# Attention blocks gathered into one stream with one PSUM bank per head, and the first two w_out_2 tiles begun together

## The chip, the cores and the metric

The kernel runs on one core of one Trainium2 chip. The metric is the device time of one execution in microseconds (us); three runs of the kernel before are shown, and one execution of it was profiled.

## What is computed

A decoder of 512 tokens and width 1024. Two layers of a first block (a feed-forward, a mixer, a feed-forward), then one layer of a second block (a mixer, a feed-forward) and a norm. The first block's mixer has, beside a pooling branch, two causal attentions of six heads each: MLA, and FoX, whose scores get a bias from a forget gate. The second block's mixer has a dilated window attention of six heads in three groups, an RWKV7 and a state space branch; their outputs are gated, summed and multiplied by `w_out_2`. Cut to what the change touches:

```python
def causal_block_attention(q, k, v, scale, log_decay_cum=None):
    def one_block(args):                     # blocks of 128 queries
        i, q_blk = args[0], args[1]
        sc = jnp.einsum('bhqd,bhkd->bhqk', q_blk, k) * scale
        if log_decay_cum is not None:
            sc = sc + c_blk[..., :, None] - log_decay_cum[..., None, :]
        sc = jnp.where(kpos[None, :] <= qpos[:, None], sc, -jnp.inf)
        p = jax.nn.softmax(sc, axis=-1)
        return jnp.einsum('bhqk,bhkd->bhqd', p, v)
def dilated_window_attention(q, k, v, window, dilation):
    scores = jnp.where(mask, jnp.einsum('bnqrhe,bnkrhe->bnrhqk', qb, kb) * (e ** -0.5), -jnp.inf)
    mx = jnp.max(scores, axis=-1, keepdims=True)
    p = jnp.exp(scores - mx)
    den = jnp.sum(p, axis=-1, keepdims=True)
    out = jnp.einsum('bnrhqk,bnkrhe->bnqrhe', p / den, vb)
    lse = mx + jnp.log(den)
merged = gates[0] * y_attn + gates[1] * y_rwkv + gates[2] * y_ssm
h = h + merged @ w_out
```

## The kernel before

Activations lie feature by feature: tiles of 128 features by 512 tokens. A weight matrix product is done for 128 output features at a time over eight k tiles of 128. Each float32 operand is split in a high and a low fp32r part, and `mm3` (lines 201 to 203) issues three matmuls for each k tile: high by high, high by low, low by high. These are the "main" matmuls, 128x512 with 128 rows. `load_w` (L394) brings a weight tile by DMA on SyncE's queue, casts its high part on ScalarE (L404) and takes the low part as a difference on VectorE (L406). There are two slots for split weights. `gemm_stream` (L410) does the output tiles one after the other; its argument `ahead=(i0, n)` lets the tiles i0 and i0+1 each do their first n k tiles before either goes on. The mixers of the first block use it; the last mixer doesn't.

The order of instructions is set when the program is built. `Sched` (L55) is a planner: every piece of work is a stream that yields an engine ("P" TensorE, "V" VectorE, "A" ScalarE, "G" GpSimd) and a cost, takes and returns slots (`acq`, `rel`: A and B are PSUM banks, s and sT the tiles for scores and turned scores) and waits for events. The piece that can start first, or of those within a short time the one with the lowest priority number, goes next. The weight product stream has priority 50 and fills what attention leaves free. Each engine then runs its instructions in that order and waits by semaphores.

First block: `attn_pair_s` (L569) takes two heads and spawns four streams `attn_block` (L522), one for each block i of 128 queries with kw = 128(i+1) keys. A stream takes two B banks for the scores of its two heads (`scores2`, L519), does `softmax_s` (the causal mask is added on VectorE, L501; the bias is added and the row maximum taken, L503; times -scale, L506; exponential with its sum on ScalarE, L508), then the reciprocal (L541), the scaling by it (L543), the transposes of its 128x128 pieces on TensorE into one B bank (L549), a copy to SBUF (L467 on ScalarE or L469 on VectorE) and the value products (L565), which add up in the pair's A bank:

```python
for j in range(nb):
    b = slice(j * P, (j + 1) * P)
    for e in range(2):
        nc.tensor.matmul(po[e], vt(e, j), sT[e][:, b], start=j == 0, stop=j == nb - 1)
```

Last mixer: `attn2` has a pair of heads in each of three groups, and in each group four streams `iteration` (L1544) of the same form, 256 keys wide in group 0 (the first block 128), 128 wide in groups 1 and 2; transposes are L1567, value products L1583. There the division comes later, so nothing is scaled ahead of the transposes. Three such streams may hold score tiles at a time.

End of the last mixer: the three branches' outputs are gated on VectorE (L1451), summed in two additions on GpSimd (L1462) and split in mgh (L476, ScalarE) and mgl (L478, VectorE), one tile of 128 features for each of eight. The `w_out_2` products take these eight as their k tiles; each output tile is added to the residual x on VectorE (L1047).

Of the kernel before, what the change touches and what calls it, by code (L numbers as in the profile page):

```python
# [9 lines left out]
F32 = mybir.dt.float32  # L10
F32R = mybir.dt.float32r
AF = mybir.ActivationFunctionType
# [141 lines left out]
class Kern:  # L154
# [341 lines left out]
    def softmax_s(self, ps, kw, s, st, bias, scale, diag, ev):  # L496

        nc = self.nc
        if diag is not None:
            yield V2  # L500
            nc.vector.tensor_add(ps[:, kw - P :], ps[:, kw - P :], diag)  # L501
        yield ("V", 0.08 + kw * 0.00104)
        nc.vector.tensor_tensor_reduce(s, ps, bias, 1.0, -3.0e38, ALU.add, ALU.max, st[0])  # L503
        yield ("rel", "B")
        yield V1
        nc.vector.tensor_scalar(st[1], st[0], -scale, None, ALU.mult)  # L506
        yield ("A", 0.28 + kw * 0.00083, 0, self.EXP)
        nc.scalar.activation(s, s, AF.Exp, bias=st[1], scale=scale, accum_out=st[2])  # L508
        yield ("sig", ev)

    def scores2(self, pair, kw, half):

        out = []
        for _ in pair:
            yield ("acq", "B")
            out.append(self.psB()[:, :kw])
        yield ("P", kw * 0.00168 * (1 if half else 2) + (0.2 if half else 0.0))
        for ps, (q, k) in zip(out, pair):
            self.nc.tensor.matmul(ps, q, k, start=True, stop=True)  # L519
        return out  # L520

    def attn_block(self, mp, pair, kw, biases, scale, diags, vt, po, done, prio, own):  # L522

        nc = self.nc
        nb = kw // P
        cs, ct = ("s", "sT") if own else ("sx", "sTx")
        ring = lambda: self.t(self.xp, "xin", (P, T), F32, 16)[:, :kw]
        yield ("acq", cs)
        ss = [self.t(mp, "s", (P, self.w_s), bufs=self.n_s)[:, :kw] if own else ring() for _ in range(2)]
        sts = [self.t(mp, "st", (P, 4), bufs=12) for _ in range(2)]  # L530
        half = pair[0][0].shape[0] == 64
        pss = yield from self.scores2(pair, kw, half)
        soft = Ev(2)

        def head(e):
            st, s = sts[e], ss[e]
            sl = [st[:, n : n + 1] for n in range(4)]
            ev = Ev()
            yield from self.softmax_s(pss[e], kw, s, sl, biases[e], scale, diags[e], ev)
            yield V1  # L540
            nc.vector.reciprocal(sl[3], sl[2])  # L541
            yield ("V", 0.135 + kw * 0.0005)
            nc.vector.tensor_scalar(s, s, sl[3], None, ALU.mult)  # L543
            yield ("acq", "B")
            pt = self.psB()[:, :kw]
            yield ("P", 0.11 * nb)
            for j in range(nb):
                b = slice(j * P, (j + 1) * P)
                nc.tensor.transpose(pt[:, b], s[:, b], self.ident)  # L549
            sT[e] = self.t(mp, "sT", (P, self.w_s), bufs=self.n_sT)[:, :kw] if own else ring()  # L550
            yield from self.copy(sT[e], pt, kw)
            yield ("rel", "B")
            yield ("sig", soft)

        sT = [None] * 2
# [5 lines left out]
        yield ("P", 0.2 + 0.115 * nb * 2)  # L561
        for j in range(nb):
            b = slice(j * P, (j + 1) * P)
            for e in range(2):
                nc.tensor.matmul(po[e], vt(e, j), sT[e][:, b], start=j == 0, stop=j == nb - 1)  # L565
# [3 lines left out]
    def attn_pair_s(self, mp, heads, vt, scale, prio, y, p, ev, own=True):  # L569
# [4 lines left out]
        done = Ev(4)  # L574
        for i in range(4):
            kw = (i + 1) * P
            bs = [bias[:, T - kw :] if diag is None else bias[:, :kw] for _, _, bias, diag in heads]
# [1717 lines left out]
```

## Time and profile before

| | |
|---|---|
| median of 3 runs | 2836.07 us (2832.83 to 2840.84) |
| profiled execution | 2837.68 us, of which the span from the first to the last instruction is 2835.9 us |
| mean granted clock of TensorE | 0.994 |
| TensorE (PE) busy | 2786.9 us, 98% |
| weight loads of TensorE (PEld) | 2220.2 us, 78% |
| VectorE (DVE) busy | 1637.9 us, 58% |
| ScalarE (ACT) busy | 1044.7 us, 37% |
| GpSimd (POOL) busy | 443.4 us, 16% |
| DMA | 277.45 MB, 98 GB/s |

A row of the profile names the engine, the line of the kernel, the operation, and what it writes and reads ("A<-xin,whi": bank tile A from xin and whi). Matmuls run into each other in the array, and the profile shows each with its own length; so two rows overlap, and the distance between two starts tells what one takes from the time. A number in brackets is the idle time ahead of an instruction and what ended it. The attentions of the first block lie at about 398 to 544 us and 1337 to 1487 us, that of the last mixer at 1987 to 2044 us, and its `w_out_2` product begins at 2411.85 us.

### The profile page before, as it was taken

The page shows a single profiled execution, that of the slowest core. Times are in us where ns is not written, and L with a number is a line of the kernel's source. Part 1 is how long each engine was busy: PE and PEld are TensorE (multiplying, and loading weights), DVE is VectorE, ACT ScalarE, POOL GpSimd, SP SyncE. Part 2 cuts the span into 40 slices and gives each one's busy share as a digit, 9 for nine tenths or more (in the row PEclk, how much of TensorE's full clock was granted, in tenths as well). Part 3 has the DMA queues.
Part 4 walks back from the last instruction along what each step waited for, and adds up shares of the span by engine and source line. Part 5 has one row for each costly group of instructions (what it writes and reads, how often), then busy time and mean ns, then how long its engine had stood idle before and what let it go on. Part 6 is the DMA issues. An engine that isn't in the chain of part 4 may idle for free. (4 is left out here: it accounts for less than half of the span.)

```text
span 2835.9 us, 33440 instructions
## 1 busy us (share of the span) xinstructions
PE 2786.9 (98%) x13036; PEld 2220.2 (78%) x13036; DVE 1637.9 (58%) x2557; ACT 1044.7 (37%) x1615; POOL 443.4 (16%) x364
## 2 busy tenths in 40 slices
PE   9999999999999999999999999998999999999998
PEld 7888877788888888887768788885677878788886
DVE  6454566654545554456665745668766756464543
ACT  4222354532223322235464324462325443332223
POOL 1010111010001200012102101124332213210012
PEclk9999999999999999999999999999999999999999
DMA  4223331222232322224123333352231116223222
GB/s 143 97 94 99 106 104 58 79 97 97 96 98 91 103 97 97 97 92 132 55 68 97 104 104 119 110 174 76 86 102 63 46 46 230 89 97 100 94 97 82
DMA packets 91974, 277.45 MB, mean 98 GB/s; under 512 B 11944, under 2 KB 13096, under 8 KB 91816
## 3 DMA queue, kind: packets, MB, share of 16 engines
q1 hardware_dynamic: 91816, 275.32, 29.6%
q8 instruction: 102, 1.67, 0.2%
q14 instruction: 56, 0.46, 0.1%
HBM read 255.87 MB, written 19.40 MB: 97 GB/s over the span
## 5 line engine op out<-in xcount | busy, mean ns | idle before, releaser
L201 PE MATMUL A<-xin,whi 128*128 128x512 f32 x2368 | 941.5, 398 | 5.6 <-ACT whi L151 5.1
L203 PE MATMUL A<-xin,wlo 128*128 128x512 f32 x2368 | 929.0, 392 | 3.6 <-DVE wlo L193 1.9
L202 PE MATMUL A<-xin,whi 128*128 128x512 f32 x2368 | 930.9, 393 | 0.0
L192 ACT CAST whi<-wraw 128x1024 fp32r<-128x1024 f32 (+1 forms) x338 | 347.7, 1029 | 1018.2 <-issue 377.9
L193 DVE TENSOR_TENSOR wlo<-wraw,whi 128x1024 fp32r<-128x1024 f32 (+1 forms) x338 | 498.8, 1476 | 82.4 <-ACT whi L192 60.4
L201 PEld LDWEIGHTS A<-xin,whi 128*128 128x128 f32 x2368 | 446.8, 189 | 118.5 <-issue 23.5
L203 PEld LDWEIGHTS A<-xin,wlo 128*128 128x128 f32 x2368 | 446.7, 189 | 98.1 <-DVE wlo L193 2.7
L202 PEld LDWEIGHTS A<-xin,whi 128*128 128x128 f32 x2368 | 446.8, 189 | 94.0 <-issue 5.3
L343 POOL TENSOR_TENSOR u<-u,g 128x512 f32<-128x512 f32 x110 | 156.4, 1422 | 1431.9 <-DVE u L341 1154.9
L202 PE MATMUL B<-hl,whi 128*128 128x512 f32 x880 | 343.2, 390 | 1.5 <-DVE hl L225 1.3
L203 PE MATMUL B<-hh,wlo 128*128 128x512 f32 x880 | 342.4, 389 | 0.0
L201 PE MATMUL B<-hh,whi 128*128 128x512 f32 x880 | 342.4, 389 | 0.0
L352 DVE SCALAR_TENSOR_TENSOR x<-B,x 128x512 f32<-128x512 f32 x120 | 83.0, 692 | 307.3 <-PE B L203 307.3
L341 DVE TENSOR_TENSOR u<-A,rb 128x512 f32<-128x512 f32 x110 | 76.0, 691 | 255.8 <-PE A L203 255.8
L404 ACT CAST whi<-wraw 128x1024 fp32r<-128x1024 f32 (+2 forms) x117 | 120.0, 1025 | 219.4 <-PE A L202 133.6
L202 PEld LDWEIGHTS B<-hl,whi 128*128 128x128 f32 x880 | 165.2, 188 | 38.2 <-DVE hl L225 4.3
L201 PEld LDWEIGHTS B<-hh,whi 128*128 128x128 f32 x880 | 165.2, 188 | 35.0
L203 PEld LDWEIGHTS B<-hh,wlo 128*128 128x128 f32 x880 | 165.2, 188 | 34.1
L406 DVE TENSOR_TENSOR wlo<-wraw,whi 128x1024 fp32r<-128x1024 f32 (+2 forms) x117 | 155.2, 1327 | 26.6 <-ACT whi L404 26.1
L337 DVE TENSOR_TENSOR g<-A,rb 128x512 f32<-128x512 f32 x110 | 75.9, 690 | 157.4 <-PE A L203 157.3
L274 POOL TENSOR_TENSOR ssum<-ssum,sq 128x512 f32<-128x512 f32 x48 | 79.3, 1653 | 366.2 <-ACT sq L273 359.7
L224 ACT CAST hh<-u 128x512 fp32r<-128x512 f32 x110 | 68.5, 623 | 158.5 <-POOL u L343 158.5
(478 smaller groups left out, 2822.0 us busy)
## 6 DMA issues: line engine op xcount, KB each, us to landing
wraw<-in_f2gu SPq DMA_DIRECT2D x88, 512.0 KB, 3.3
wraw<-in_f1gu SPq DMA_DIRECT2D x86, 512.0 KB, 3.3
wraw<-in_w_in SPq DMA_DIRECT2D x76, 512.0 KB, 3.4
wraw<-in_f3gu SPq DMA_DIRECT2D x44, 512.0 KB, 3.3
wraw<-in_f1db SPq DMA_DIRECT2D x32, 448.0 KB, 3.3
wraw<-in_f2db SPq DMA_DIRECT2D x32, 448.0 KB, 3.3
wraw<-in_w_out SPq DMA_DIRECT2D x24, 512.0 KB, 3.4
wraw<-in_f1da SPq DMA_DIRECT2D x16, 512.0 KB, 3.3
```

The lines of the kernel that those rows point to most:

```text
L192: nc.scalar.copy(hi[:, b], raw[:, b])
L193: nc.vector.tensor_sub(lo[:, b], raw[:, b], hi[:, b])
L201: mm(ps, wh, xh, start=first, stop=False)
L202: mm(ps, wh, xl, start=False, stop=False)
L203: mm(ps, wl, xh, start=False, stop=last)
L274: (nc.vector if k == NK - 1 else nc.gpsimd).tensor_add(self.ssum, self.ssum, sq)
L337: nc.vector.tensor_mul(g, pg, rb)
L341: nc.vector.tensor_mul(u, pu, rb)
L343: nc.gpsimd.tensor_mul(u, u, g)
L352: nc.vector.scalar_tensor_tensor(self.x[o], ps, scale, self.x[o], ALU.mult, ALU.add)
L404: nc.scalar.copy(hi[:, :width], raw[:, :width])
L406: nc.vector.tensor_sub(lo[:, :width], raw[:, :width], hi[:, :width])
```

## The change

First, `attn_block` takes several blocks of queries as one stream. Their scores lie side by side in one bank for each head: blocks 0 and 1 together (128 + 256 columns), block 2 and block 3 alone. Mask, bias and maximum, exponential and scaling remain one instruction for each block; the product with -scale and the reciprocal are done once for the stream; the transposes of all its pieces go into one bank and are copied once (`turned`); the value products of its blocks follow each other. Second, the last mixer's attention does the same: group 0 in two streams of two blocks, groups 1 and 2 in one stream of four blocks each; score tiles become 512 wide, four instead of six, and two streams instead of three may hold them. Third, `gemm_stream` of the last mixer gets `ahead`: the first two w_out_2 tiles do seven k tiles each before either does its eighth. The core of the diff:

```diff
-    def softmax_s(self, ps, kw, s, st, bias, scale, diag, ev):
+    def softmax_s(self, ps, subs, s, sts, scale, diag):
+
 
         nc = self.nc
-        if diag is not None:
-            yield V2
-            nc.vector.tensor_add(ps[:, kw - P :], ps[:, kw - P :], diag)
-        yield ("V", 0.08 + kw * 0.00104)
-        nc.vector.tensor_tensor_reduce(s, ps, bias, 1.0, -3.0e38, ALU.add, ALU.max, st[0])
+        for c, bias, st in subs:
+            kw = c.stop - c.start
+            if diag is not None:
+                yield V2
+                nc.vector.tensor_add(ps[:, c.stop - P : c.stop], ps[:, c.stop - P : c.stop], diag)
+            yield ("V", 0.08 + kw * 0.00104)
+            nc.vector.tensor_tensor_reduce(s[:, c], ps[:, c], bias, 1.0, -3.0e38, ALU.add, ALU.max, st[0])
         yield ("rel", "B")
         yield V1
-        nc.vector.tensor_scalar(st[1], st[0], -scale, None, ALU.mult)
-        yield ("A", 0.28 + kw * 0.00083, 0, self.EXP)
-        nc.scalar.activation(s, s, AF.Exp, bias=st[1], scale=scale, accum_out=st[2])
-        yield ("sig", ev)
-
-    def scores2(self, pair, kw, half):
+        nc.vector.tensor_scalar(sts[1], sts[0], -scale, None, ALU.mult)
+        for c, bias, st in subs:
+            yield ("A", 0.28 + (c.stop - c.start) * 0.00083, 0, self.EXP)
+            nc.scalar.activation(s[:, c], s[:, c], AF.Exp, bias=st[1], scale=scale, accum_out=st[2])
+
+    def scores2(self, pairs, w, half):
...
+        for c, pair in pairs:
+            for ps, (q, k) in zip(out, pair):
+                self.nc.tensor.matmul(ps[:, c], q, k, start=True, stop=True)
...
+    def turned(self, s, w, out):
+
+        yield ("acq", "B")
+        pt = self.psB()[:, :w]
+        yield ("P", 0.11 * w / P)
+        for b in range(0, w, P):
+            self.nc.tensor.transpose(pt[:, b : b + P], s[:, b : b + P], self.ident)
+        t = out()[:, :w]
+        yield from self.copy(t, pt, w)
+        yield ("rel", "B")
+        return t
+
...
+    def attn_block(self, mp, heads, blocks, scale, vt, po, done, prio, own):
...
+        ends = [sum(n + 1 for n in blocks[: x + 1]) * P for x in range(len(blocks))]
+        cols = [slice(e - (n + 1) * P, e) for n, e in zip(blocks, ends)]
+        w = ends[-1]
...
+            n = len(blocks)
+            yield from self.softmax_s(pss[e], subs, s, (st[:, 0, :n], st[:, 1, :n]), scale, diag)
...
+            nc.vector.reciprocal(st[:, 3, :n], st[:, 2, :n])
+            for x, c in enumerate(cols):
+                yield ("V", 0.135 + (c.stop - c.start) * 0.0005)
+                nc.vector.tensor_scalar(s[:, c], s[:, c], st[:, 3, x : x + 1], None, ALU.mult)
...
+            sT[e] = yield from self.turned(s, w, out)
...
+        yield ("P", 0.2 + 0.23 * w / P)
+        for i, c in zip(blocks, cols):
+            for j in range(i + 1):
+                b = slice(c.start + j * P, c.start + j * P + P)
+                for e in range(2):
+                    y = po[e * 64 : e * 64 + 64, i * P : i * P + P]
+                    nc.tensor.matmul(y, vt(e, j), sT[e][:, b], start=j == 0, stop=j == i)
...
-        done = Ev(4)
-        for i in range(4):
+        done = Ev(3)
+        for i, blocks in enumerate(((0, 1), (2,), (3,))):
+            it = self.attn_block(mp, heads, blocks, scale, vt, po, done, prio + 0.02 * i, own)
...
-        self.n_s, self.n_sT, self.w_s, self.p_load = 6, 4, 256, 1.05
+        self.n_s, self.n_sT, self.p_load = 4, 4, 1.05
...
-        sch = self.sch = Sched(self.preload, E2, N2, W2, A=4, B=4, s=3, sT=2, sq=1, zb=4, gt=2, j=2, jx=1, av=2, u=4, q=5, gl=6, B2=2, raw=3, w=2)
+        sch = self.sch = Sched(self.preload, E2, N2, W2, A=4, B=4, s=2, sT=2, sq=1, zb=4, gt=2, j=2, jx=1, av=2, u=4, q=5, gl=6, B2=2, raw=3, w=2)
...
-            sch.add(self.gemm_stream(items), 50, "g")
+            sch.add(self.gemm_stream(items, None if stop else (len(order) + NK, NK - 1)), 50, "g")
...
+            los = [max(0, i - 1) if g == 0 else i for i in blocks]
+            ends = [sum(n - lo + 1 for n, lo in zip(blocks[: x + 1], los)) * P for x in range(len(blocks))]
+            cols = [slice(e - (n - lo + 1) * P, e) for n, lo, e in zip(blocks, los, ends)]
+            w = ends[-1]
...
+                yield from self.softmax_s(pss[s], subs, ts[s], (st[:, s, g, 0, a:b], ng[:, n + a : n + b]), 0.125, None)
+                sT[s] = yield from self.turned(ts[s], w, lambda: self.t(ap, "sT", (P, T), bufs=self.n_sT))
...
+            sets = ((0, 1), (2, 3)) if g == 0 else ((0, 1, 2, 3),)
+            dn = Ev(len(sets))
+            for i, blocks in enumerate(sets):
```

TensorE, first layer, first FoX pair, behind the scores of blocks 0 and 1 (fk, fq: keys and queries; s: scores; sT: turned scores; c_ident: the identity that transposes). Before:

```order
L549 MATMUL B_2890<-c_ident_141,s_2826 128x128 x2
L565 MATMUL A_2819<-sT_2880,vt_2799 64x128
L565 MATMUL A_2819<-sT_2882,vt_2799 64x128
L549 MATMUL B_2895<-c_ident_141,s_2827 128x128 x2
L519 MATMUL B_2905<-fk_2740,fq_2700 128x384
L519 MATMUL B_2906<-fk_2740,fq_2700 128x384
L565 MATMUL A_2819<-sT_2909,vt_2799 64x128
L565 MATMUL A_2819<-sT_2915,vt_2799 64x128
```

Changed:

```order
L533 MATMUL B_2905<-c_ident_141,s_2820 128x128 x3
L533 MATMUL B_2910<-c_ident_141,s_2821 128x128 x3
L533 MATMUL B_2914<-c_ident_141,s_2826 128x128 x3
L533 MATMUL B_2920<-c_ident_141,s_2827 128x128 x3
L201 MATMUL A_2872<-xin_2529,whi_2795 128x512
L202 MATMUL A_2872<-xin_2530,whi_2795 128x512
L203 MATMUL A_2872<-xin_2529,wlo_2796 128x512
L586 MATMUL A_2819<-sT_2918,vt_2799 64x128
L586 MATMUL A_2819<-sT_2924,vt_2799 64x128
```

The four blocks' transposes, value products and scores alternated before; now the transposes of both heads of blocks 0, 1 and 2 stand together, three main matmuls follow, and twelve value products (to A_2819, the first two shown) run without a break up to the scores of block 3. The 384-wide scores of block 2, between the value products before, have moved up behind those of blocks 0 and 1.

TensorE at the first w_out_2 tiles (A_18607 and A_18645 before, A_18319 and A_18351 now; mgh and mgl are the k tiles, mgh_18627 before and mgh_18339 now the eighth). Before:

```order
L201 MATMUL A_18607<-mgh_18586,whi_18563 128x512
L202 MATMUL A_18607<-mgl_18587,whi_18563 128x512
L203 MATMUL A_18607<-mgh_18586,wlo_18564 128x512
L201 MATMUL A_18607<-mgh_18627,whi_18563 128x512
L202 MATMUL A_18607<-mgl_18628,whi_18563 128x512
L203 MATMUL A_18607<-mgh_18627,wlo_18564 128x512
L201 MATMUL A_18645<-mgh_18298,whi_18605 128x512
```

Changed:

```order
L203 MATMUL A_18351<-mgh_18298,wlo_18318 128x512
L201 MATMUL A_18319<-mgh_18339,whi_18275 128x512
L202 MATMUL A_18319<-mgl_18340,whi_18275 128x512
L203 MATMUL A_18319<-mgh_18339,wlo_18276 128x512
L201 MATMUL A_18351<-mgh_18339,whi_18317 128x512
L202 MATMUL A_18351<-mgl_18340,whi_18317 128x512
L203 MATMUL A_18351<-mgh_18339,wlo_18318 128x512
L201 MATMUL A_18401<-mgh_18010,whi_18377 128x512
L202 MATMUL A_18401<-mgl_18011,whi_18377 128x512
L201 MATMUL A_18434<-mgh_18010,whi_18399 128x512
L202 MATMUL A_18434<-mgl_18011,whi_18399 128x512
L203 MATMUL A_18401<-mgh_18010,wlo_18378 128x512
```

Before, the first tile's eighth k tile follows its seventh directly, and the second tile begins behind it. Now the second tile's first seven k tiles stand ahead of the first tile's eighth, and the third and fourth tile (A_18401, A_18434) begin behind the pair.

VectorE, first layer, third FoX pair, blocks 0 and 1 (st: a row's maximum, sum and reciprocal; vm: values in token order). Before:

```order
L541 RECIPROCAL st_3609<-st_3609 128x1
L506 TENSOR_SCALAR st_3616<-st_3616 128x1
L819 TENSOR_TENSOR x_3642<-A_3624,c_rope_2585 128x512
L543 TENSOR_SCALAR s_3607<-s_3607,st_3609 128x128
L469 COPY vm_2604<-B_3649 128x384
L541 RECIPROCAL st_3610<-st_3610 128x1
L541 RECIPROCAL st_3615<-st_3615 128x1
L541 RECIPROCAL st_3616<-st_3616 128x1
L543 TENSOR_SCALAR s_3608<-s_3608,st_3610 128x128
L543 TENSOR_SCALAR s_3613<-s_3613,st_3615 128x256
L543 TENSOR_SCALAR s_3614<-s_3614,st_3616 128x256
```

Changed:

```order
L567 RECIPROCAL st_3577<-st_3577 128x2
L469 COPY vm_2604<-B_3618 128x384
L570 TENSOR_SCALAR s_3575<-s_3575,st_3577 128x128
L570 TENSOR_SCALAR s_3575<-s_3575,st_3577 128x256
L567 RECIPROCAL st_3578<-st_3578 128x2
L469 COPY vm_2604<-B_3632 128x384
L570 TENSOR_SCALAR s_3576<-s_3576,st_3578 128x128
L570 TENSOR_SCALAR s_3576<-s_3576,st_3578 128x256
L506 ISA s_3582,st_3584<-B_3586,cb_3089 128x384
```

The first head's transposes need the scaling of s_3607 before, of both parts of s_3575 now. One copy of vm stood ahead of the second head's first scaling; now there are two, and the second head's scalings (s_3576) follow the first head's second part.

## Rows read from the trace of the kernel before

**Rows 1.** Page, busy time of TensorE: us, share of the span, instructions.

```profile
PE 2786.9 (98%) x13036; PEld 2220.2 (78%) x13036; DVE 1637.9 (58%) x2557; ACT 1044.7 (37%) x1615; POOL 443.4 (16%) x364
```

**Rows 2.** Timeline of TensorE, first w_out_2 tile: start, duration, engine, line, operation.

```profile
2411.85 0.39 PE L201 MATMUL A<-mgh,whi 128*128 128x512 f32 x1
...
2416.38 0.39 PE L203 MATMUL A<-mgh,wlo 128*128 128x512 f32 x1
2419.44 0.50 PE L201 MATMUL A<-mgh,whi 128*128 128x512 f32 x1 [2.67 <-ACT mgh L476]
2420.17 0.49 PE L202 MATMUL A<-mgl,whi 128*128 128x512 f32 x1 [0.23 <-DVE mgl L478]
...
2424.37 0.40 PE L201 MATMUL A<-mgh,whi 128*128 128x512 f32 x1
```

**Rows 3.** Table of waits of TensorE: us in total, times, longest.

```profile
PE B L549 <- DVE s L543: 6.1, 4, 2.1
...
PE A L201 <- ACT mgh L476: 2.7, 1, 2.7
...
PE B L519 <- DVE ast L503: 1.2, 1, 1.2
...
PE B L549 <- DVE st L506: 0.8, 2, 0.4
```

**Rows 4.** Table by windows, TensorE: length, busy, granted clock, DMA share, GB/s.

```profile
465.00:468.40 3.40, 3.40 (x16) 0.52 0.31 118
...
2421.00:2424.40 3.40, 3.40 (x10) 0.50 0.16 27
```

**Rows 5.** Timeline of TensorE, scores between main matmuls, first layer.

```profile
397.96 0.40 PE L203 MATMUL A<-xin,wlo 128*128 128x512 f32 x1
398.29 0.93 PE L519 MATMUL B<-fk,fq 64*128 64x128 f32 x8
399.14 0.50 PE L201 MATMUL A<-xin,whi 128*128 128x512 f32 x1
399.48 0.39 PE L202 MATMUL A<-xin,whi 128*128 128x512 f32 x1
```

**Rows 6.** Timeline of TensorE, attention runs next to each other, first layer.

```profile
404.62 0.44 PE L565 MATMUL A<-sT,vt 128*64 128x128 f32 x4
404.99 0.44 PE L549 MATMUL B<-c_ident,s 128*128 128x128 f32 x2
405.35 0.92 PE L519 MATMUL B<-fk,fq 64*128 64x384 f32 x4
406.20 0.66 PE L565 MATMUL A<-sT,vt 128*64 128x128 f32 x8
406.79 1.13 PE L519 MATMUL B<-fk,fq 64*128 64x512 f32 x4
407.85 0.50 PE L201 MATMUL A<-xin,whi 128*128 128x512 f32 x1
```

**Rows 7.** Timeline of TensorE, value products between main matmuls, last mixer.

```profile
2018.50 0.50 PE L202 MATMUL A<-xin,whi 128*128 128x512 f32 x1
2018.84 0.55 PE L1583 MATMUL A<-avT,sT 128*128 128x64 f32 x4
...
2019.52 0.39 PE L201 MATMUL A<-xin,whi 128*128 128x512 f32 x1
```

**Rows 8.** Timelines of TensorE and VectorE, second and third FoX pair, first layer.

```profile
461.22 2.06 DVE L406 TENSOR_TENSOR wlo<-wraw,whi 128x1024 fp32r<-128x1024 f32 x1
...
464.45 0.55 PE L549 MATMUL B<-c_ident,s 128*128 128x128 f32 x3 [2.11 <-DVE s L543]
...
493.41 0.55 DVE L469 COPY vm<-B 128x384 f32<-128x384 f32 x1
```

**Rows 9.** Timelines of VectorE and ScalarE at the first w_out_2 tile.

```profile
2415.62 2.00 DVE L406 TENSOR_TENSOR wlo<-wraw,whi 128x1024 fp32r<-128x1024 f32 x1
...
2420.70 1.05 ACT L404 CAST whi<-wraw 128x1024 fp32r<-128x1024 f32 x1 [1.31 <-PE A L202]
```

More of the change, by code (lines that the diff above doesn't have):

```diff
@@ L513, in scores2 @@
+    def scores2(self, pairs, w, half):
         out = []
-        for _ in pair:
+        for _ in range(2):
             yield ("acq", "B")
[L516 to L519, printed above, removed]
-        return out
-    def attn_block(self, mp, pair, kw, biases, scale, diags, vt, po, done, prio, own):
+            out.append(self.psB()[:, :w])
+        yield ("P", w * 0.00168 * (1 if half else 2) + (0.2 if half else 0.0))
+        for c, pair in pairs:
+            for ps, (q, k) in zip(out, pair):
+                self.nc.tensor.matmul(ps[:, c], q, k, start=True, stop=True)
+        return out
@@ L526, in attn_block @@
         cs, ct = ("s", "sT") if own else ("sx", "sTx")
-        ring = lambda: self.t(self.xp, "xin", (P, T), F32, 16)[:, :kw]
+        ring = lambda: self.t(self.xp, "xin", (P, T), F32, 16)
         yield ("acq", cs)
[L529 to L533, printed above, removed]
+        ss = [self.t(mp, "s", (P, self.w_s), bufs=self.n_s) if own else ring() for _ in range(2)]
@@ L535, in head @@
+        sts = [self.t(mp, "st", (P, 4, 2), bufs=12) for _ in range(2)]
+        pairs = [
+            (c, [(q[:, i * P : i * P + P], k[:, : i * P + P]) for q, k, _, _ in heads]) for i, c in zip(blocks, cols)
+        ]
+        pss = yield from self.scores2(pairs, w, heads[0][0].shape[0] == 64)
+        soft, sT = Ev(2), [None] * 2
         def head(e):
             st, s = sts[e], ss[e]
-            sl = [st[:, n : n + 1] for n in range(4)]
-            ev = Ev()
-            yield from self.softmax_s(pss[e], kw, s, sl, biases[e], scale, diags[e], ev)
@@ L540, in head @@
-            yield V1
[L541 to L550, printed above, removed]
@@ L551, in head @@
-            yield from self.copy(sT[e], pt, kw)
-            yield ("rel", "B")
+            bias, diag = heads[e][2:]
+            subs = []
+            for x, (i, c) in enumerate(zip(blocks, cols)):
+                kw = i * P + P
+                b = bias[:, T - kw :] if diag is None else bias[:, :kw]
+                subs.append((c, b, [st[:, f, x : x + 1] for f in range(3)]))
+            n = len(blocks)
+            yield from self.softmax_s(pss[e], subs, s, (st[:, 0, :n], st[:, 1, :n]), scale, diag)
@@ L1552, in iteration @@
             r = [slice(s * 64, s * 64 + 64) for s in range(2)]
-            ts = [self.t(ap, "s", (P, 256), bufs=self.n_s)[:, :kw] for _ in range(2)]
-            pair = [(q[x, i * P : i * P + P], k[x, lo * P : (i + 1) * P]) for x in r]
-            pss = yield from self.scores2(pair, kw, True)
+            ts = [self.t(ap, "s", (P, T), bufs=self.n_s) for _ in range(2)]
+            pairs = [
+                (c, [(q[x, i * P : i * P + P], k[x, lo * P : i * P + P]) for x in r]) for i, lo, c in zip(blocks, los, cols)
+            ]
@@ L1568, in head @@
-                sT[s] = self.t(ap, "sT", (P, 256), bufs=self.n_sT)[:, :kw]
-                yield from self.copy(sT[s], pt, kw)
-                yield ("rel", "B")
+                n = (g * 2 + s) * 4
+                subs = []
+                for i, c in zip(blocks, cols):
+                    m = m0[:, 256 - (c.stop - c.start) :] if g == 0 else (m1, m2)[g - 1]
+                    subs.append((c, m, (st[:, s, g, 0, i : i + 1], ng[:, n + i : n + i + 1], st[:, s, g, 1, i : i + 1])))
+                a, b = blocks[0], blocks[-1] + 1
```

50 lines of the change are left out of this document (12 added, 38 removed).

## The prediction

> **What bounds the kernel.** I read the page's busy times first. TensorE is busy 98% of the span [rows 1], but the main matmuls overlap in the records: 21 of them in a row start 0.2265 us apart (2411.85 to 2416.38, [rows 2]) while one lasts 0.39 us. So the busy share can't show lost time; the distance from start to start can, and every price below is taken from it. Then I read the table of waits: of the idle time that TensorE shows in the two places of the change, 6.1 us are transposes of the attention waiting for the scaled scores of VectorE (four times, longest 2.1); 1.2 us a score matmul waiting for a softmax in the last mixer, and 2.7 us the first w_out_2 tile waiting for the last merged operand [rows 3]. Third, the table by windows: TensorE ran at a granted clock of 0.50 to 0.52, its level of 1.2 GHz, in 3.4 us behind the longest attention wait and behind the w_out_2 wait [rows 4]; ahead of each it had stood idle. The chain that decides the time is TensorE's own order. A change helps if it takes work, distance or waits out of that order.
>
> **Part 1: fewer, longer runs of attention matmuls.** The change leaves the number of matmuls as it is and gathers them. A run is a group of scores (S), of transposes (T) or of value products (V) with nothing else between. Counted in the two orders, each layer of the first block has 21 S and 26 V runs before, 15 and 19 after; the last mixer has 8 S and 17 V before, 4 and 4 after. That is 6+6+4 = 16 S and 7+7+13 = 27 V runs less, 43 in all. What does a run cost beyond its matmuls?
>
> - S between main matmuls [rows 5]: from L203 at 397.96 to L202 at 399.48 it is 1.52 us; without the scores that would be two steps, 0.45, so the run costs 1.07. The columns cost 0.41 us per 1000: 512-wide scores take 1.06 (406.79 to 407.85), 384-wide ones 0.85 (405.35 to 406.20), for 512 columns more [rows 6]. The run has 1536 columns (four scores of 128, four of 256), 0.63. Left: 0.44 a run. The same with neighbours that are attention too: 0.85 - 0.63 = 0.22 [rows 6].
> - V: four take 0.37 (404.62 to 404.99), eight 0.59 (406.20 to 406.79) [rows 6], so 0.055 each, and 0.15 a run among neighbours of its kind. Between main matmuls [rows 7]: 2018.50 to 2019.52 is 1.02, less two steps 0.57, less four products 0.35 a run.
> - T: the number of T runs falls too, by 6 in each layer and 18 in the last mixer. Two transposes between V and S took 0.36 [rows 6], which leaves at most 0.14 a run if a transpose takes what two V do. I cost them at nothing, and keep 30 x 0.14 = 4.2 us as an upper end.
>
> I take 0.35 for each of the 43, the price of V between main matmuls, since 27 of them are V: **-15.0 us**. Lower end 43 x 0.15 = 6.5, upper end 43 x 0.44 = 18.9 (23.1 with T). VectorE loses 64 small instructions (24 reciprocals, 40 products with -scale); TensorE doesn't wait for most of them, so I count nothing, and where it does wait they can only help.
>
> **Part 2: the waits inside attention.** Here the sign is open. A merged stream's first transpose waits for more VectorE work than before; against that, the planner now puts more main matmuls ahead of it. In the first FoX pair there are 33 (7.5 us) between the scores and the first transpose instead of 15 (3.4 us), so its wait of 0.4 (two such in the table, [rows 3]) should go. In the second pair, the 2.11 us wait came from a weight split (L406, 2.06 us) ahead of a scaling [rows 8]. In the new order the split is still there; behind it now stands the copy of the first turned head, for which six V wait: I expect the same 2 us, and the same drop of the clock behind it. In the third pair the wait was about 0.94 (6.1 less twice 2.1, halved, [rows 3]); the first head's second scaling and one more copy of vm (0.55, [rows 8]) now stand ahead of the transposes, so I add 0.9. MLA: its pairs come with few main matmuls between; I add 0.5 a layer. Last mixer: the wait of 1.2 us was for the next bank; now the transposes wait for two exponentials behind the scan's VectorE work, +0.4. Per layer -0.4 + 0.9 + 0.5 = +1.0, twice +2.0, +0.4 in the last mixer, and I allow for one more drop of the clock at 1.7 us (its price is worked out in part 3): together **+4 us**. Ends: all of these waits gone (6.1 + 1.2) with one drop of 1.7, -9; or four more waits with a drop each, +14.
>
> Each block has banks of its own before, and the scores of blocks 0 and 1 go out as one run of eight matmuls in 0.85 us (398.29 to 399.14, [rows 5]); VectorE can begin on block 0 while block 1 is still written. The Trainium skill, page "PSUM — Partial Sum Buffer", section "PSUM bank collisions raise a hardware error", has two engines kept off one bank and quadrant at the same time, with guards by bank and not by address; no run here shows it. By that rule a merged stream's softmax starts up to 0.85 us later; covered by the main matmuls the sum stays as it is, uncovered it is that of rival A.
>
> **Part 3: two w_out_2 tiles begin together.** Before, the first tile does seven of its eight k tiles and waits for the last merged operand. From its L203 at 2416.38 to L201 at 2424.37 there are 13 steps [rows 2]; they took 7.99 us instead of 13 x 0.2265 = 2.94, so 5.05 us are lost: the waits of about 3.3, and 1.7 at half clock behind them (4.20 us from 2420.17 to 2424.37 for 11 steps, 2.49). After, the second tile's seven k tiles stand there: 21 matmuls, 4.76 us, longer than the waits. But new waits come:
> - The second tile's low half comes from the split that ends at 2417.62 (L406, 2.00 us from 2415.62 [rows 9]); its first L203 would be due at 2417.06. Wait 0.56.
> - Both weight slots now come free at the end of the pair, one right after the other. The cast of the third tile starts 0.53 us behind the first tile's last L202 (2420.17 to 2420.70 [rows 2, 9]) and takes 1.05, so it is there after 1.58; TensorE needs it after five steps, 1.13. Wait 0.45. The fourth tile's cast follows it, another 1.05, with only two matmuls placed ahead of that: wait 0.6. The split behind two evictions: some 0.4.
>
> Together 2.0 us are given back: **-3.0 us**. Ends: -4.5 (only the first wait) and 0 (the waits bring the clock down again, 1.7, and a split of 2 us instead of 1.2).
>
> **Sum.** -15.0 + 4.0 - 3.0 = -14.0. The profiled execution took 2837.68 us, so it would take 2823.7. The median of the runs lies 1.6 lower, at 2836.07; against it I forecast **2822.0 us**. What a measurement here can tell from no change is about 0.3%, 8.5 us: below 2827.6 is faster, above 2844.6 slower.
>
> **Rivals.**
> - A, the saved distance comes back as waiting (same). There are 16 merged streams: one in each of 12 pairs, four in the last mixer. If each begins its softmax later by a whole score run, 0.85 us [rows 5], since its first block has to wait for its second, and nothing covers that, 16 x 0.85 = 13.6 comes back: 2822 + 13.6 = 2835.6. For it: transposes waited for VectorE before. Against: 3.4 to 7.5 us of main matmuls stand between scores and transposes in the first FoX pair. Chance 0.22. The Trainium skill's rule on banks, named above, would give this at worst.
> - B, slower: VectorE becomes the bound inside attention. Place: the first transpose of every merged stream. If a weight split stands ahead of its scalings each time, as in the second FoX pair, each costs 2.1 of wait [rows 8] and 1.7 at half clock, 3.8 us. 16 x 3.8 = 61, less three that are there already, 11, is +50; less the 18 of parts 1 and 3: +32, 2868. It decides from five new such waits (18 / 3.8), and is slower by over 0.3% from seven (26.5 / 3.8). For it: L406 took 2.06 just there. Against: such transposes waited only four times before [rows 3], in 48 blocks of pairs. Chance 0.09.
> - C, the waits go as well. Merged scalings and longer cover take out 7.3 us of waits and one drop of the clock, so part 2 is -9 instead of +4: 2809. For it: the first FoX pair's cover doubles. Chance 0.14.
> - D, the pair of tiles gives nothing (weights late, clock down again) and parts 1 and 2 hold: 2825; it is faster all the same. Chance 0.05. That the change doesn't do what it says is ruled out by the order: the runs are gathered and the two tiles interleaved.
>
> **How the numbers follow.** The forecast has 0.50, with 2812 to 2832 as its own range. Faster: the forecast's 0.50 less 0.04 for its slow end, C and D, together 0.65. Same: A and that slow end, 0.26. Slower: B, 0.09. The range reaches from 2808 (C, just taken in) to 2838 (A with a few us more); B and the tails of A and C are left out.
>
> **What would show it.** Part 1: the score line fewer and longer runs, the busy time of the main lines unchanged, and from the first score to the last V of each layer's attention about 4 us less, in the last mixer about 6. Part 2: the table of waits has the transposes (L533) waiting for L570 with about 6 to 8 us in all, and V (L586) for a copy of about 2. Part 3: no wait for mgh, but waits for whi and wlo at the third and fourth w_out_2 tile of 0.5 to 1 us. I am wrong if the waits for VectorE grow beyond 20 us (B), if the score and V runs are as dear as before per matmul (A), or if the granted clock falls in many new places.

## The result and the profile after

The changed kernel took 2817.89 us (median of six runs, 2814.71 to 2819.99); the kernel before took 2833.15 us in the six runs beside them (2830.48 to 2840.84). The ratio is 0.9938, 95% interval 0.9927 to 0.9950: 14 to 21 us faster. The forecast was 2822.0, 14 us faster, with a range of 2808 to 2838.

The page of the profiled execution of the changed kernel (busy us, share, instructions; compare [rows 1]):

```profile
span 2817.6 us, 33309 instructions
...
PE 2771.2 (98%) x13036; PEld 2216.3 (79%) x13036; DVE 1631.4 (58%) x2496; ACT 1027.0 (36%) x1567; POOL 443.1 (16%) x364
```

The span went from 2835.9 to 2817.6, 18.3 us; TensorE's busy share says 98% in both and tells nothing. The number of its records is the same, so the time came out of the distance from one start to the next. The table of waits of TensorE (compare [rows 3]; us in total, times, longest):

```profile
PE B L533 <- DVE s L570: 6.3, 8, 2.6
...
PE A L1599 <- DVE sT L469: 3.7, 3, 2.7
PE B L1303 <- DVE FT L1288: 3.2, 3, 1.5
PE A L203 <- DVE wlo L406: 2.1, 2, 1.7
...
PE B L533 <- ACT s L512: 1.2, 4, 0.5
PE A L1942 <- POOL sx L1938: 0.8, 1, 0.8
...
PE B L524 <- DVE sx L1916: 0.7, 1, 0.7
PE A L586 <- DVE sT L469: 0.7, 1, 0.7
...
PE A L201 <- ACT whi L404: 0.4, 2, 0.2
```

The transposes of the first block (L533) wait as long as before (6.3 us against 6.1, in eight waits instead of four); the wait for mgh is gone, with small ones for weights in its place; and a wait of 2.7 us is new: value products of the last mixer (L1599) for a copy of turned scores. Two waits outside the change got shorter: the RWKV's for FT, and the state space branch's for sw and sx of GpSimd. Before they were:

```profile
PE B L1287 <- DVE FT L1272: 3.9, 4, 2.1
...
PE B L1304 <- DVE FT L1272: 1.6, 1, 1.6
...
PE A L1926 <- POOL sw L1921: 1.4, 1, 1.4
...
PE A L1927 <- POOL sx L1923: 1.0, 1, 1.0
```

The w_out_2 product in the timeline of TensorE (compare [rows 2]):

```profile
2401.68 0.50 PE L203 MATMUL A<-mgh,wlo 128*128 128x512 f32 x1 [0.45 <-DVE wlo L406]
...
2407.87 0.50 PE L201 MATMUL A<-mgh,whi 128*128 128x512 f32 x1 [0.24 <-ACT whi L404]
...
2408.82 0.50 PE L201 MATMUL A<-mgh,whi 128*128 128x512 f32 x1 [0.21 <-ACT whi L404]
```

The first is the second tile's first L203, the others begin the third and the fourth tile. These are three of the places that the prediction named, each with some tenths of a microsecond. In the table by windows, the last row here, TensorE is at its full level of 2.4 GHz there (granted clock 1.00). The four rows above it are all its stretches at 1.2 GHz (0.50) ahead of the last 15 us (compare [rows 4]):

```profile
394.90:398.30 3.40, 3.40 (x9) 0.50 0.17 70
1401.80:1405.20 3.40, 3.40 (x9) 0.50 0.02 5
1907.00:1910.40 3.40, 3.40 (x9) 0.50 0.12 47
1992.30:1995.70 3.40, 3.40 (x8) 0.50 0.00 0
2400.00:2410.00 10.00, 9.11 (x37) 1.00 0.16 54
```

Where the 18.3 us came from, by the starts of the same instructions in the two traces (us; "half clock" is the time lost in the stretches at 1.2 GHz, half of their length):

| stretch | before | after | difference |
|---|---|---|---|
| up to the first score of layer 1 | 398.29 | 400.01 | +1.7 (a half-clock stretch at 394.9) |
| layer 1: first score to last value product | 149.38 | 143.16 | -6.2 (1.7 of it half clock) |
| from there to the first score of layer 2 | 789.71 | 788.97 | -0.7 |
| layer 2: first score to last value product | 149.36 | 144.99 | -4.4 |
| from there to the last mixer's first score | 500.18 | 494.94 | -5.2 (3.4 of it half clock) |
| last mixer: first score to the first w_out_2 matmul | 424.93 | 423.78 | -1.1 |
| w_out_2 | 48.35 | 45.34 | -3.0 (1.7 of it half clock) |
| rest, up to the last matmul | 365.76 | 366.48 | +0.7 |

Inside layer 1, the time from each matmul's start to the next one's, without idle time and half clock (the "distance" of the text below), added up by kind (us, runs):

| kernel | scores, runs | value products, runs | transposes, runs | idle |
|---|---|---|---|---|
| before | 23.15, 21 | 17.96, 26 | 14.21, 32 | 4.05 |
| after | 20.76, 15 | 16.86, 19 | 13.90, 26 | 3.36 |

The same number of matmuls in fewer runs: 2.39 us less for 6 runs of scores (0.40 each), 1.10 for 7 of value products (0.16 each). Three more main matmuls stand in this stretch after the change, 0.7 us that the next stretch no longer has.

### The profile page after: what moved, and what is told of

Read it like the earlier page. It is cut to its first block, busy times and chain, and to the rows that moved or that the text cites. A ratio compares the mean times of both kernels' runs of the same rounds, so it can differ in the third digit from the quotient of the medians.

```text
span 2817.6 us, 33309 instructions
## 1 busy us (share of the span) xinstructions
PE 2771.2 (98%) x13036; PEld 2216.3 (79%) x13036; DVE 1631.4 (58%) x2496; ACT 1027.0 (36%) x1567; POOL 443.1 (16%) x364
## 5 line engine op out<-in xcount | busy, mean ns | idle before, releaser
L203 PE MATMUL A<-xin,wlo 128*128 128x512 f32 x2368 | 927.6, 392 | 3.6 <-DVE wlo L193 1.9
L201 PEld LDWEIGHTS A<-xin,whi 128*128 128x128 f32 x2368 | 446.2, 188 | 119.3 <-issue 23.9
L203 PEld LDWEIGHTS A<-xin,wlo 128*128 128x128 f32 x2368 | 445.9, 188 | 98.8 <-DVE wlo L193 3.2
L203 PE MATMUL B<-hh,wlo 128*128 128x512 f32 x880 | 342.4, 389 | 0.0
L203 PEld LDWEIGHTS B<-hh,wlo 128*128 128x128 f32 x880 | 165.2, 188 | 34.1
```

The source lines that it names most:

```text
L201: mm(ps, wh, xh, start=first, stop=False)
L203: mm(ps, wl, xh, start=False, stop=last)
```

## The experiments

**The three parts apart.** Theory 1 is the prediction's sum: runs that are saved pay by the run. e1 has the first block's merging alone, e2 the last mixer's, e3 the pair of tiles.

e1, against the changed kernel:

```diff
-            sch.add(self.gemm_stream(items, None if stop else (len(order) + NK, NK - 1)), 50, "g")
+            sch.add(self.gemm_stream(items), 50, "g")
...
-            sets = ((0, 1), (2, 3)) if g == 0 else ((0, 1, 2, 3),)
+            sets = ((0,), (1,), (2,), (3,))
```

(with three streams and six score tiles of 256 columns, as before). Expected:

> Only the first block's attention is merged (blocks 0 and 1 as one stream, in both layers); the last mixer has its single-block streams and no pair of w_out_2 tiles. Theory 1 (each run of scores or value products that is saved is worth about 0.35 us on TensorE): 12 S and 14 V runs fewer, 26 x 0.35 = 9 us faster than before, the waits for VectorE changed by less than 2 us. Rival A (the saved distance comes back as waiting): within 2 us of before. Rival C (the waits are what pays): no fewer than 5 us of waits gone in the table of waits.

Measured: 2825.05 us against 2835.65, ratio 0.9959, interval 0.9947 to 0.9970; 8.5 to 15 us faster, 10.6 by the medians. Its layer 1 shows the same 20.76 and 16.84 us of scores and value products as the changed kernel, and its table of waits more transposes' waits than before, not fewer:

```profile
PE B L533 <- DVE s L570: 7.3, 8, 2.6
```

All idle time in the two attentions together fell by 0.8 us, which can't pay for 10; rivals A and C fall for the first block. But the whole trace has 5.0 us less idle time than that of before (34.1 against 39.0), nearly the 5 us that rival C asks for: 4.5 of it lies behind the second layer's attention, where e1 merges nothing; the work there is the same, and only the moments at which it meets are others. Over the whole trace, up to the last w_out_2 matmul, the distance fell by 9.4 us, the 9 of theory 1; 5.2 less idle time, 1.7 more half clock and 0.5 behind w_out_2 make the 12.3 us by which the two profiles differ.

e2, against the changed kernel:

```diff
-        done = Ev(3)
-        for i, blocks in enumerate(((0, 1), (2,), (3,))):
+        done = Ev(4)
+        for i, blocks in enumerate(((0,), (1,), (2,), (3,))):
```

and no pair, as in e1. Expected:

> Only the last mixer's attention is merged; first block and w_out_2 as before. Theory 1: 4 S and 13 V runs fewer, -6.0 us, and +4.4 us of new waits that the changed kernel's trace shows there (the longest, 2.7 us, value products that wait for a copy of turned scores on VectorE): together about 1.5 us faster than before. Rival (the half-clock stretch of 10.2 us ahead of the attention in the profile of before, 3.4 us in that of the changed kernel, goes because of the merging): 3.4 us more, about 5 us faster, and its profile shows 3.4 us at half clock there. Rival A: 4 us slower, the new waits alone.

Measured: 2835.22 us, ratio 0.9992 (0.9984 to 1.0000): at most 4.5 us faster, by the medians 0.4. Its mixer, from the first score to the first w_out_2 matmul, took 423.89 us, as in the changed kernel (423.78; before 424.93). The waits are there with nothing else changed:

```profile
PE A L1599 <- DVE sT L469: 3.7, 3, 2.7
PE B L533 <- ACT s L512: 1.0, 4, 0.4
```

The half-clock stretch ahead of the attention was 10.2 us before, 6.8 in e1 and e2, 10.2 in e3, 3.4 in the changed kernel; it goes with none of the three edits.

e3, against the kernel before:

```diff
-            sch.add(self.gemm_stream(items), 50, "g")
+            sch.add(self.gemm_stream(items, None if stop else (len(order) + NK, NK - 1)), 50, "g")
```

Expected:

> The kernel before with only the first two w_out_2 tiles begun together. Theory 1: 5.05 us lost there before; the changed kernel's trace shows waits of 0.45, 0.24 and 0.21 us and no drop of the clock, so some 4 us faster; with the steps that the waits take beyond their idle time 3 us, as forecast. Rival D (weights late, clock down again): within 1 us of before.

Measured: 2834.09 us, ratio 0.9992 (0.9983 to 1.0001): 2.3 us, interval from none to 5. The trace is sharper: the w_out_2 product takes 45.34 us in e3, in the changed kernel and in every later kernel with the pair (45.33 to 45.38), 48.35 before and 48.40 in e2. Nothing else in its trace moved by more than a few tenths, but for a half-clock stretch ahead of the first attention, so rival D falls by the trace; the interval alone would not exclude it. By their ratios the three parts are worth 11.6, 2.3 and 2.3 us, together 16.2, where the whole change has 17.6 (0.9938). The distances do add up: 9.4, 2.8 and -0.1 us less in e1, e2 and e3, 11.1 in the changed kernel. Idle time and clock don't: 5.2, 1.3 and 2.0 us less idle time against 2.8, and 1.7, 1.7 and 0 us more lost at half clock against 5.1 less. So the sum of the ratios shows less than it seems to.

**What holds the last mixer back (e7).** The new wait of 2.7 us, in the timelines of VectorE and TensorE of the changed kernel:

```profile
1986.11 1.78 DVE L1934 TENSOR_TENSOR sx<-sx,sw 128x512 f32<-128x512 f32 x1
1987.81 1.75 DVE L1186 SCALAR_TENSOR_TENSOR w<-w,vecs,w 128x512 f32<-128x512 f32 x1
1989.48 0.68 DVE L469 COPY sT<-B 128x512 f32<-128x512 f32 x1
...
1990.21 0.99 PE L1599 MATMUL A<-avT,sT 128*128 128x64 f32 x7 [2.71 <-DVE sT L469]
```

The transposes were done at 1986.3; the planner had put one of the two copies on VectorE, behind instructions of the other branches that take 1.8 us each. e7 puts all such copies on ScalarE:

```diff
-        yield from self.copy(t, pt, w)
+        yield ("A", 0.07 + w * 0.0008)
+        self.nc.scalar.copy(t, pt)
```

> The changed kernel, with every copy of turned scores on ScalarE (the planner chose ScalarE or VectorE for each). Theory 1: the value products of the last mixer's group waited 2.7 us for a copy that stood on VectorE behind three instructions of 1.8 us each; that wait goes, and 0.7 us in each second FoX pair: 3 to 4 us faster than the changed kernel. Rival: ScalarE has its exponentials and casts in front, the copies come later and other waits take their place: the same or slower than the changed kernel.

Measured: 2811.77 us, ratio to before 0.9914 (0.9901 to 0.9926), 21 to 28 us faster than before and 6 us under the changed kernel's median: the fastest kernel here. In its last attention one kind of wait is left:

```profile
PE B L533 <- ACT s L512: 1.0, 4, 0.4
```

From the first score to the first w_out_2 matmul it takes 417.02 us instead of 423.78: 4.6 us of waits less in the attention (0.7 us more behind it), no half-clock stretch behind them (1.7), and the rest distance. In the first block there is 0.3 to 0.4 us a layer in it. That is more than the 3 to 4 us expected: over the whole trace the idle time fell by 6.5 us, and the expectation left out the clock (1.7).

**The copies without the merging (e8).** The kernel before with copies on ScalarE and the pair:

```diff
-            yield from self.copy(sT[e], pt, kw)
+            yield ("A", 0.07 + kw * 0.0008)
+            nc.scalar.copy(sT[e], pt)
```

(the same in `iteration`). Expected:

> The kernel before, single-block streams, with the copies of turned scores on ScalarE and the pair of w_out_2 tiles; nothing merged. Theory 1: 3 us for the pair and 1 us at most of waits, about 4 us faster than before. Rival (the copies alone give most of what the kernel with merged streams and copies on ScalarE has gained, 24 us): 10 us or more faster than before.

Measured: 2833.76 us, ratio 0.9992 (0.9982 to 1.0001). That is what e3 has with the pair alone: the copies give nothing that can be measured where the blocks stand alone; what they remove is a wait that the merging brings.

**Runs made shorter again (e4, e5).** e4 asks for TensorE once for each score matmul, e5 once for each transpose, so that the planner puts main matmuls between:

```diff
-        yield ("P", w * 0.00168 * (1 if half else 2) + (0.2 if half else 0.0))
         for c, pair in pairs:
             for ps, (q, k) in zip(out, pair):
+                yield ("delay", 0.5)
+                yield ("P", (c.stop - c.start) * 0.00084 * (1 if half else 2) + (0.1 if half else 0.0))
```

> The changed kernel, but the planner asks for TensorE once for each score matmul, half a microsecond apart, so that main matmuls go between them; the same matmuls, banks and VectorE work. By its order there are 49 runs of scores (34 in the changed kernel) and 48 of value products (42). Theory 1: 21 runs x 0.35 = 7 us slower than the changed kernel, with like waits. Rival A (the distance is not what costs): no slower than 2 us, or slower only by what the table of waits gains.

```diff
-        yield ("P", 0.11 * w / P)
         for b in range(0, w, P):
+            yield ("delay", 0.5)
+            yield ("P", 0.11)
```

> The changed kernel, but the transposes are asked for one by one, half a microsecond apart. By its order 130 runs of transposes instead of 61, 57 of value products instead of 42, 42 of scores instead of 34. Theory 1, with transposes as runs at nothing: 23 x 0.35 = 8 us slower. At the upper bound of the prediction for a run of transposes, 0.14, another 9.7: 18 us slower. Rival A: within 2 us of the changed kernel.

Measured: e4 2846.16 us, 1.0035 (1.0022 to 1.0048); e5 2839.37, 1.0011 (1.0002 to 1.0020), where the changed kernel has 0.9938. That is 28 and 21 us slower than the changed kernel: the distance does cost, but theory 1 had 7 and 8, and neither time settles the price of a run. Taken apart as above, up to the last w_out_2 matmul, e4 has 16.6 us more distance than the changed kernel, 7.9 more idle time and 3.4 more half clock; e5 has 7.0, 7.2 and 10.2. So e5's distance is about what theory 1 had; what the theory lacked is the waits and the clock, since an order with other runs has other waits. In e5 the transposes of layer 1 take 13.15 us in 59 runs, less than the 13.90 in 26 runs of the changed kernel, so a run of transposes has no price of its own, and the 18 us of the upper bound, near as it is to the 21, is not what happened. What grew: idle time (3.36 to 5.85), half clock (3.4), value products in 25 runs (18.70) and the main matmuls between.

In e4 the scores alone grew from 20.76 to 26.04 us for eight runs more. All of that is FoX, whose scores have 64 rows: 7.68 to 13.41 us. MLA's, with 128 rows, went from 13.08 to 12.64 in four runs more, so theirs cost nothing more. The timeline shows why FoX paid (start, duration; the next start tells what it took):

```profile
402.29 0.81 PE L525 MATMUL B<-fk,fq 64*128 64x384 f32 x2
403.03 0.50 PE L201 MATMUL A<-xin,whi 128*128 128x512 f32 x1
```

and in the changed kernel:

```profile
400.77 0.81 PE L524 MATMUL B<-fk,fq 64*128 64x384 f32 x4
401.51 0.50 PE L201 MATMUL A<-xin,whi 128*128 128x512 f32 x1
```

A 384-wide score has two records, so the first row is one head's and the second is both heads'. One head's score alone takes 0.74 us; two heads' scores, on rows 0 to 63 and 64 to 127, take 0.74 together. e4 put main matmuls between the two heads and paid twice.

**Must the two heads' scores be neighbours? (e10)**

```diff
-        for c, pair in pairs:
-            for ps, (q, k) in zip(out, pair):
-                self.nc.tensor.matmul(ps[:, c], q, k, start=True, stop=True)
+        for e, ps in enumerate(out):
+            for c, pair in pairs:
+                self.nc.tensor.matmul(ps[:, c], *pair[e], start=True, stop=True)
```

> The changed kernel with the scores of a stream in another order: all blocks of the first head, then all blocks of the second; the same matmuls in the same runs. In the kernel with the scores asked for one by one, six records of 128, 384, 128 columns took 1.07 us where the heads' matmuls no longer stood side by side, 0.66 us per 1000 columns behind the fixed part, instead of 0.41. Theory 2 (two heads' score matmuls, on the two halves of the rows, cost less when they follow each other): the run of blocks 0 and 1 in the first FoX pair gets 0.2 to 0.4 us longer, and the scores of a layer 0.6 to 1.2 us; the whole 2 to 3 us slower than the changed kernel. Rival (the order of the heads doesn't matter, only the number of runs): the scores of a layer take the same time within 0.2 us.

One run, 2824.89 us against 2835.49 in the run of before beside it. In the first block the run of blocks 0 to 2 takes 1.51 us, 1.50 in the changed kernel, and the scores of the layer 20.78 us against 20.76.

```profile
398.04 1.58 PE L524 MATMUL B<-fk,fq 64*128 64x128 f32 x12
399.55 0.50 PE L201 MATMUL A<-xin,whi 128*128 128x512 f32 x1
```

Theory 2 falls as it was put: with one other score between them the heads still run side by side. But the edit reaches the last mixer too, where a stream of groups 1 and 2 has four blocks, so that three other scores stand between a block's two heads. There a run takes 1.64 us instead of 1.09, in both groups. First e10, then the changed kernel:

```profile
2000.37 1.71 PE L524 MATMUL B<-ak,aq 64*128 64x128 f32 x16
2002.01 0.50 PE L201 MATMUL A<-xin,whi 128*128 128x512 f32 x1
```

```profile
1999.22 1.16 PE L524 MATMUL B<-ak,aq 64*128 64x128 f32 x16
2000.31 0.50 PE L201 MATMUL A<-xin,whi 128*128 128x512 f32 x1
```

So the order of the heads does matter where three scores stand between. The profile of e10 is 5.5 us longer than the changed kernel's, and 5.1 of that is the clock: 23.9 us at half clock instead of 13.6.

**Fewer small VectorE instructions (e6).**

```diff
-        yield V1
-        nc.vector.tensor_scalar(sts[1], sts[0], -scale, None, ALU.mult)
         for c, bias, st in subs:
+            yield V1
+            nc.vector.tensor_scalar(st[1], st[0], -scale, None, ALU.mult)
...
-            yield V1
-            nc.vector.reciprocal(st[:, 3, :n], st[:, 2, :n])
             for x, c in enumerate(cols):
+                yield V1
+                nc.vector.reciprocal(st[:, 3, x : x + 1], st[:, 2, x : x + 1])
```

> The changed kernel with the product with -scale and the reciprocal done for each block again (64 more small VectorE instructions); streams, banks and runs stay gathered (by its order two runs of scores and two of value products fewer). Theory 1: these instructions are not on the path, within 2 us of the changed kernel. Rival (the smaller number of small VectorE instructions is what pays): 64 x 0.06 to 0.15 = 4 to 10 us slower.

Measured: 2824.96 us, 0.9961 (0.9949 to 0.9974): 7 us above the changed kernel's median, in the rival's range; the two intervals just touch. So the time does not bear out theory 1, which had it within 2 us. The profiles are only 3.9 us apart. The added waits are small: 0.9 and 0.6 us of idle time in the two layers, and 0.4 less from the last mixer's first score to w_out_2. The distance is 1.5 us less, with two runs of scores fewer. The rest is the clock: stretches at half clock ahead of the last 15 us add up to 23.9 us instead of 13.6, 5.1 us lost, one of them (6.8 us, at 1330) ahead of the second attention, where the two kernels' work is the same. So these instructions are worth 1.5 us of waits in the first block; whether the clock's part belongs to them is open (e10, with none of them, has as much of it).

## Why the prediction was right, point by point

- **The sum.** The forecast was 14 us faster; the medians say 15.3, the ratio 17.6, the two profiles 18.3. That it came so near is in part luck, for two of its terms missed in opposite directions. Taken from the two traces, stage by stage as in the table above (us):

| term | forecast | measured |
|---|---|---|
| part 1, distance | -15.0 | -11.8 |
| part 2, waits | +2.4 | -0.8 |
| part 2, clock | +1.7 | -3.4 |
| part 3, w_out_2 | -3.0 | -3.0 |
| behind w_out_2 | 0 | +0.7 |

- **What bounds the kernel**: right. All that counts is in the distance of TensorE's starts, its waits and its clock; the distances of e1, e2 and e3 add up.
- **Part 1, runs, -15.0 us.** Right in the first block, in kind and size: 13 runs a layer were costed at 4.55 us; without idle time and half clock a layer's attention got 3.8 us shorter with 0.7 us more of main matmuls in it, so 4.5 (scores 2.4, value products 1.1, the rest 1.0). By kind the price was 0.40 for scores (FoX's 0.41, MLA's 0.39) and 0.16 for value products, not 0.35 for both. e1 has the same. Transposes at nothing: right (e5). Where the prediction counts score matmuls and value products in rows, it counts records; each of these matmuls leaves two (96 records for 48 scores in a layer). Its prices are by record throughout, so the sum doesn't change.
- The last mixer's share, 17 x 0.35 = 6.0, **was mis-sized**. The step that failed is "less four products 0.35 a run" [rows 7]: it took the 0.055 us of a value product from the first block [rows 6] for the last mixer's. But there the turned scores are the weights, 128x128 for 64 columns, and a record takes 0.12: twelve 1.25 us (1980.52 to 1981.77, changed kernel), sixteen 1.74 (1981.97 to 1983.71, e7). The row's 0.57 is then almost all products, 0.08 is left for the run, and 13 runs are worth 1, not 4.6. By the trace the mixer's distance fell by about 3 (it got 1.1 shorter in spite of the waits named below, +4.4 and -2.4), and the value products have no share in that: they take 6.47 us in 17 runs before and 6.85 in 4 after, while the scores went from 6.78 to 4.79. The rows of these two runs, changed kernel and e7:

```profile
1980.52 1.45 PE L1599 MATMUL A<-avT,sT 128*128 128x64 f32 x12
1981.77 0.48 PE L201 MATMUL A<-xin,whi 128*128 128x512 f32 x1
```

```profile
1981.97 1.93 PE L1600 MATMUL A<-avT,sT 128*128 128x64 f32 x16
1983.71 0.48 PE L201 MATMUL A<-xin,whi 128*128 128x512 f32 x1
```

- **Part 2, waits, +4 us.** By place: the first FoX pair's 0.4 us went, as said. The second pair kept its 2 us (0.68 + 1.60 in layer 1, 2.55 in layer 2). The third pair got shorter (0.95 and 0.29 before, 0.67 and 0.19 after) where 0.9 more was forecast: the added copy of vm and scaling were covered. MLA kept 0.2 of 0.3, where 0.5 more was forecast. That is -0.7 and -0.4 in the two layers. The last mixer's attention has 5.60 us of waits instead of 1.16, +4.4 where +0.4 was forecast: the prediction looked at the exponentials and not at the engine on which the copies of turned scores would stand, and e7 shows that it was this. The RWKV part behind it lost 2.4 us of waits and the state space part ahead of it 1.5, which the prediction had not looked at. Without these two the waits came to +3.3 against +2.4 forecast, but from other places; with them they fell by 0.8.
- The clock was allowed one more drop, +1.7. There were fewer: 23.9 us at half clock ahead of the last 15 us before, 13.6 after, 5.1 us less lost, 1.7 of it at w_out_2. That is as much as the difference between 14 and 18 us in the profiles. It isn't shown to be the change's doing. 3.4 us of it is the stretch ahead of the last mixer's attention, which went from 10.2 to 3.4. TensorE's order there is the same in every trace here, and three patterns occur. In before, e3, e5 and e8 the clock stays up behind a wait of 1.3 us for a weight from DMA; then come 2.1 to 2.3 us of waits for sw and sx, and the 10.2 us at half clock behind them. In the changed kernel, e4, e6 and e10 the clock falls behind the wait for the weight, for 3.4 us, and 0.8 to 0.9 us of waiting for sx is left. In e1, e2 and e7 it falls there for 6.8 us, and no such wait is left. So the state space part's 1.5 us belongs to the same pattern. Which kernel gets which pattern, and whether each execution of it does, one profile of each can't tell.
- **Blocks that share a bank**, up to 0.85 us for each merged stream: in the first FoX pair of layer 1 VectorE's first mask (L501, now L504) began 0.52 us behind the first score before (398.81 against 398.29) and 0.96 behind it now (400.97 against 400.01), so the softmax did start later, by 0.44. 33 main matmuls cover it, and no transpose there waits at all. Rival A fell in e1. The rule of the Trainium skill, page "PSUM — Partial Sum Buffer", section "PSUM bank collisions raise a hardware error", keeps two engines off one bank and quadrant at the same time and would have given rival A at worst; no run here shows what happens without that guard.
- **Part 3, pair of tiles, -3.0 us**: right, 48.35 to 45.34, with the clock's drop gone and three waits in the places named (0.45, 0.24 and 0.21 idle against 0.56, 0.45 and 0.6); the fourth, 0.4 for a split behind two evictions, did not come.
- Rival B: five new waits of 2 us with a drop each would have decided; there is one, in the last mixer, and it cost what B says, 2.7 and 1.7. Rival C came partly true, through the clock, the RWKV and the state space part. Rival D fell by e3's trace.

## What to carry to other kernels

Where matmuls of one kind are strewn among others, price a run by the distance of starts, for each shape by itself and in its own place: here a run of scores was worth 0.40 us between the two orders, one of value products 0.16 in the first block and nothing in the last mixer, one of transposes nothing. Such a price holds for the order that it was read from: in e4 MLA's scores in four more runs cost nothing. When small streams are merged, look at the engine on which each remaining step will stand: one copy on VectorE behind other branches' work gave back what the last mixer's merging had saved (2.7 us of waiting and 1.7 of clock against some 3 of distance). An idle hole of two tiles can be filled with the next tile's work, but count what the shared weight slots cost at its end.

## What the hardware showed that was not expected

- Two heads' scores with 64 rows each run side by side: 0.74 us for two 384-wide ones, 0.74 for one alone (e4). One other score between them doesn't hinder this (e10, first block: 1.51 us for the run against 1.50), three do in part (e10, last mixer: 1.64 against 1.09), and main matmuls between do (e4: 5.7 us of FoX's scores in layer 1). The Trainium skill, page "TensorEngine Tiling (Array Packing)", section "When to Use Tiling", has twofold row tiling for a contraction of 64; these rows agree.
- Ahead of the last 15 us a stretch at 1.2 GHz is 3.4, 6.8 or 10.2 us long in these traces, and in a stage whose work is the same it stands behind different waits, with different lengths. Two kernels compared by one profile each can differ by 5 us through this alone (e10 and the changed kernel), so the stages are compared with it taken out. The runs of one kernel differ by it as well: the mean granted clock of e1's five runs lies between 0.993 and 0.996, and the fastest of them, 2821.29 us, is the one at 0.996.
